# A decoder layer on one core: weights handed over tile by tile, and TensorE's order taken from the scheduler

## The chip, the core and the metric

The kernel runs on one core of a Trainium2 chip. A core has a matrix engine (TensorE, PE in the profile; its weight loads are listed as PEld), three engines for elementwise work (VectorE or DVE, ScalarE or ACT, GpSimd or POOL) and SyncE (SP), which issues all the DMAs of this kernel. Each engine takes its instructions in its own fixed order and waits on semaphores for the others. Matrix products land in PSUM, 8 banks of 128 x 512 float32; everything else works in SBUF. The metric is the device time of one execution in microseconds (us).

## The reference, cut to what matters

```python
def reference(x, c, w_ada, b_ada, g_attn, w_in, b_f, sinks, w_out,
              g_mlp, w_up, conv_w, conv_b, w_down, g_final):
    mod = jax.nn.silu(c) @ w_ada + b_ada
    sh1, sc1, ga1, sh2, sc2, ga2 = jnp.split(mod, 6, axis=-1)
    h = modulate(rms_norm(x, g_attn), sh1, sc1)
    x = x + ga1[:, None, :] * hybrid_mixer(h, w_in, b_f, sinks, w_out)
    h2 = modulate(rms_norm(x, g_mlp), sh2, sc2)
    x = x + ga2[:, None, :] * conv_glu_mlp(h2, w_up, conv_w, conv_b, w_down)
    return rms_norm(x, g_final)
```

x is 2048 rows of 1024 float32. The mixer projects h with w_in (1024 x 2312) into queries, keys and values of 8 heads with a sliding window of 128 and of 8 heads of forgetting attention over all earlier rows, and multiplies the heads by w_out (1024 x 1024). The MLP is h2 @ w_up (1024 x 5632), a causal convolution of width 3, silu(g) * a, and a product with w_down (2816 x 1024). w_ada is 1024 x 6144.

## The kernel before

**Tiles and stages.** The 2048 rows are cut into four blocks n = 0..3 of 512. For each, s1(n) makes the projections (L276 for the first groups of block 0, L623 for the columns q and k, L651 for the values), s2(n) the attention, and s3(n) the rest: the product with w_out (L1183), the normalised rows h2 turned by transposes (L525), the product with w_up (L1301) and the one with w_down (L1183 again). Each dense product is made of three, of a high and a low part of either side: in a row of the profile, `hh,wh`, `hl,wh`, `hh,wl`.

**Attention.** A unit of forgetting attention (fox_unit) makes scores s (L968), the maximum of each column by a transpose mt (L993), spreads it over rows by mb (L1000), takes exponentials on ACT and differences on DVE (L1018, L1019), sums by a transpose lt (L1039), and multiplies the probabilities, split into ph and pl (L728, L729), with the values into o (L1063, L1066); yo (L1072 to L1074) is its output. There are 8 such units for block 0 and 1, one a head, and 16 for block 2 and 3. The sliding window has its scores at L798, its transposes at L840 and its products at L851 and L852, with yo at L867 and L868.

**Weights.** `want` lists all weight tiles in the order of use, `feed` (L409) loads them some tiles ahead of use from the ten buffers of the tag w, and `split_w` makes wh on ACT (L378) and wl on DVE (L379). Some tiles, once split, are stored to DRAM (L406) and loaded as wkh and wkl for later blocks (L399). A tile of w_up or of w_in's columns is 128 columns of all 1024 rows: SBUF [128, 8, 128]. A tile of w_out, w_down and of w_in's first groups is 256 rows of up to 512 columns: [128, 2, 512]. The values' tiles are two or three blocks of rows of 320 or 328 columns. w_ada comes in 96 tiles of 128 x 512: 32 by `ada_pair` (L191), each of two pieces of 256 columns, at the start, and 64 by `ada_chunk` (L181) while the first attention runs; DVE adds them up (L199, L201), and PE sums them over the partitions (L256, and L209 in `mod_cols`). h2 needs what L209 gives.

**What sets the order.** The last lines of the kernel body `merge` a dense generator (s1, s3) with an attention generator (s2): for each step of dense products that is written out, attention steps are written out as a ratio and a table of gaps allow. So s2(1) is written between the steps of s3(0), s2(2) between those of s1(3) and s3(1), and s2(3) between those of s3(2). The framework's scheduler then plans the whole program with a model of each instruction's duration, and decides the order on each engine; an instruction that is written earlier goes first if both are ready in the plan. For PE this is switched off, for the whole kernel, by

```python
    ctx.enter_context(tc.manual_schedule(engines={mybir.EngineType.PE}))
```

(L117): PE executes its instructions as they were written. Within s1(0)'s first groups DVE and SP are held to the written order too (L608), and DVE at the very end (L1432).

Of the kernel before, what the change touches and what calls it, by code (L numbers as in the profile page):

```python
# [15 lines left out]
P = 128  # L16
D = 1024
# [3 lines left out]
KT = D // P  # L21
# [9 lines left out]
FG = 3  # L31
NW = 1 + (FG > 0)
# [38 lines left out]
def tile_decoder_layer(  # L71
# [4 lines left out]
    w_ada: bass.AP,  # L76
    b_ada: bass.AP,
    g_attn: bass.AP,
    w_in: bass.AP,
    b_f: bass.AP,  # L80
    sinks: bass.AP,
    w_out: bass.AP,
# [8 lines left out]
    nc = tc.nc  # L91
# [22 lines left out]
        return t[:, :w]  # L114

    nc.scalar.preload_act_table_set("exp_and_others")
    ctx.enter_context(tc.manual_schedule(engines={mybir.EngineType.PE}))  # L117

    def side_ps(w=512):
        t = pa.tile([P, 512], F32, tag="s", name="sd", bufs=3)  # L120
# [10 lines left out]
        out=tri, in_=tri, pattern=[[1, P]], compare_op=ALU.is_ge, fill=0.0,  # L131
# [5 lines left out]
        out=cmask, in_=cmask, pattern=[[1, P]], compare_op=ALU.is_ge, fill=-BIG,  # L137
# [8 lines left out]
        out=dist, in_=dist, pattern=[[-1, 256]], compare_op=ALU.is_ge, fill=1e35,  # L146
# [3 lines left out]
        out=dist, in_=dist, pattern=[[1, 256]], compare_op=ALU.is_gt, fill=1e35,  # L150
# [30 lines left out]
    def ada_chunk(i, accs):  # L181
        acc = ap.tile([P, 512], F32, tag="act", name="acc")
        for k in range(KT):
            w = ap.tile([P, 512], F32, tag="act", name="wada")
            with behind():
                nc.sync.dma_start(w, w_ada[k * P : (k + 1) * P, i * 512 : (i + 1) * 512])
            ada_step(acc, w, k)
            yield
        accs.append(acc)

    def ada_pair(i, k, acc):  # L191
        w = at.tile([P, 2, 256], F32, tag="t", name="wada2", bufs=NT)
        src = w_ada[k * P : (k + 1) * P, 0 : 2 * D].rearrange("p (s n) -> p s n", s=2)
        nc.sync.dma_start(w, src[:, :, i * 256 : (i + 1) * 256])
        ada_step(acc, w.rearrange("p s n -> p (s n)"), k)

    def ada_step(acc, w, k):
        if k == 0:
            nc.vector.tensor_scalar(acc, w, cc[:, 0:1], 1.0, ALU.mult, ALU.mult)  # L199
        else:  # L200
            nc.vector.scalar_tensor_tensor(  # L201
                acc, w, cc[:, k : k + 1], acc, ALU.mult, ALU.add
            )
# [32 lines left out]
    def first_groups():  # L236
# [48 lines left out]
        for i in range(5):  # L285
            sums = None
            if i < 4:
                sums = ap.tile([P, 512], F32, tag="act", name="acc")
            for k in range(KT):
                if i < 4:  # L290
                    ada_pair(i, k, sums)
                if i > 0 and k == 1:
                    shape(i - 1, prev)
                    if i > 1:
                        for m in range(1, NW):
                            products(2 * i - 4, [m])
                            products(2 * i - 3, [m])
                if i > 0 and k in (3, 5):
                    kk = 2 * (i - 1) + (k - 3) // 2
                    modulate_one(*h_pair(hh, hl, kk), xts[kk], kk, 0, 0)  # L300
                    if k == 5:
                        products(kk - 1, [0])
                        products(kk, [0])
            prev = sums
            if i == 0:
                feed(3, 2)
# [23 lines left out]
    def prologue_later():  # L330
        for chunks in ((4, 5), range(6, 10), (10, 11)):
            accs = []
            for i in chunks:
                yield from ada_chunk(i, accs)
            for _ in range(MY):
                yield
            if chunks == (4, 5):
                mod_rows(accs, 16, 0)
                late["gate"] = True
            elif chunks == (10, 11):  # L340
                mod_rows(accs, 40, 1)
            else:
                mod_cols(accs, 24)
                nc.vector.scalar_tensor_tensor(
                    scl[:, 8:16], mod[:, 32:40], 1.0, late["gml"], ALU.add, ALU.mult
                )
                late["mod"] = True
# [34 lines left out]
    def behind():  # L382
        return tc.issue_after(flow["last"]) if "last" in flow else nullcontext()
# [6 lines left out]
    def want(shape, srcs, key=None, use=None):  # L390
        if use is not None:
            mode[len(reqs)] = (key, use)
        reqs.append((shape, srcs))
# [42 lines left out]
    def want_s1(n):  # L436
        if n == 0:
            for k2 in range(KT // 2):
                for c0, c1 in ((768, 1280), (1280, 1280 + FG * P))[:NW]:
                    want([P, 2, c1 - c0], [((slice(None),), w_in[  # L440
                        k2 * 256 : (k2 + 1) * 256, c0:c1
                    ].rearrange("(a p) n -> p a n", p=P))])
        cols = []
        for i in range(4):
            if n > 0:
                cols += [768 + i * P, 1280 + i * P]
            elif i >= FG:
                cols += [1280 + i * P]
        def want_cols(cols):
            for col in cols:  # L450
                want([P, KT, P], [((slice(None),), w_in[:, col : col + P].rearrange(
                    "(k p) n -> p k n", p=P))])

        want_cols(cols)
        for ch in range(2):
            wd = 320 + 8 * ch
            for k0, nk in ((0, 3), (3, 3), (6, 2)):
                src = w_in[k0 * P : (k0 + nk) * P, :].rearrange("(k p) n -> p k n", p=P)
                a = slice(None)
                if ch == 0:  # L460
                    srcs = [
                        ((a, a, slice(0, 128)), src[:, :, 640:768]),
                        ((a, a, slice(128, 320)), src[:, :, 1792:1984]),
                    ]
                else:
                    srcs = [((a, a, a), src[:, :, 1984:2312])]
                want([P, nk, wd], srcs)
        want_cols([i * P for i in range(5)])

    def use_of(n, key):  # L470
        if key not in first_use:
            first_use[key] = KEEP[len(first_use) % len(KEEP)]
        at0 = first_use[key]
        return "load" if n > at0 else "store" if n == at0 else "raw"
# [3 lines left out]
    def want_rows(src, order, n, name):  # L478
        for half in range(2):
            for k2 in [k // 2 for k in order if k % 2 == 0]:  # L480
                key = f"{name}{half}_{k2}"
                want([P, 2, 512], [((slice(None),), src[
                    k2 * 256 : (k2 + 1) * 256, half * 512 : (half + 1) * 512
                ].rearrange("(a p) n -> p a n", p=P))], key, use_of(n, key))

    def want_s3(n):
        want_rows(w_out, OUT_ORDER, n, "o")
        calm.update(range(len(reqs) - CB, len(reqs) + CN))
        for f in range(NF):
            for ci in (f, NF + f):  # L490
                key = f"u{ci}"
                want([P, KT, P], [((slice(None),), w_up[:, ci * P : (ci + 1) * P].rearrange(
                    "(k p) n -> p k n", p=P))], key, use_of(n, key))
        want_rows(w_down, range(NF), n, "d")

    def sumsq(row, out, junk=None):
# [1002 lines left out]
    for (kind, n), alt in zip(order, (0, 1, 1, 2, 3, 3, 4, 5)):  # L1499
        if kind == "s1":  # L1500
            want_s1(n)
        else:
            want_s3(n)
        alts.extend([alt] * (len(reqs) - len(alts)))
# [21 lines left out]
_INS = [  # L1526
    "x", "c", "w_ada", "b_ada", "g_attn", "w_in", "b_f", "sinks", "w_out",
    "g_mlp", "w_up", "conv_w", "conv_b", "w_down", "g_final",
]
_OUTS = [((1, S, D), "float32")]  # L1530


# [27 lines left out]
```

## Time and profile before

| | |
|---|---|
| median of 3 runs | 2754.8 us (2751.72 to 2756.76) |
| the profiled execution | 2755.67 us, span 2754.0 us |
| DMA queue of SP | 424316 packets, 585.79 MB, busy 65.8% of 16 engines' span |
| packets under 2 KB | 272756 |

The span is the time from the first to the last instruction. A row of the waits reads: who waited, for whom, then the sum in us, the number of waits and the longest. In a timeline row the time of the start and the duration come first, and in brackets stands how long the engine had been idle and what ended that.

### The profile page before, as it was taken

The numbers are of one execution on the slowest core, as the hardware profiler recorded it, in microseconds if no ns is written. First come the engines' busy times: TensorE is split into PE (matmuls) and PEld (weight loads), VectorE is DVE, ScalarE is ACT, GpSimd is POOL, SyncE is SP. The second block draws the span as 40 slices with busy tenths as digits, with TensorE's granted clock in tenths as the row PEclk, the third lists the DMA queues.
The fourth block names the chain that finished last, engine by engine and source line by source line (L and its number), as shares of the span: only waits on it lengthen the run. The fifth ranks groups of instructions, "written<-read, shape, count | busy, mean of one in ns | idle before, by whom it ended". The sixth has DMA issues, their size and how long they took to land.

```text
span 2754.0 us, 38503 instructions
## 1 busy us (share of the span) xinstructions
PE 2566.3 (93%) x12852; PEld 2168.5 (79%) x12852; DVE 1930.8 (70%) x3813; ACT 1491.7 (54%) x3085; POOL 93.1 (3%) x171
## 2 busy tenths in 40 slices
PE   7999888799989999988999999989999999999998
PEld 5878786677877877877788887878888887788887
DVE  6467656789878657776888865879989876344433
ACT  5456564565556666556555665576666666422222
POOL 0001000100000000000000000100000000000000
PEclk9999999899999999999999999999999999999999
DMA  7967579756646786675667779735555576655564
GB/s 234 296 181 234 153 216 306 237 178 200 198 150 201 218 263 204 210 245 166 211 225 228 236 255 300 274 119 179 182 186 180 180 243 218 249 196 196 188 228 183
DMA packets 424515, 588.26 MB, mean 214 GB/s; under 512 B 32380, under 2 KB 272756, under 8 KB 424316
## 3 DMA queue, kind: packets, MB, share of 16 engines
q1 hardware_dynamic: 424316, 585.79, 65.8%
q8 instruction: 102, 1.67, 0.3%
q14 instruction: 97, 0.79, 0.1%
HBM read 440.95 MB, written 144.71 MB: 213 GB/s over the span
## 4 chain that ended last, share of the span: by engine, by line
PE 75%; DVE 8%; DMA 7%; ACT 5%; issue 2%; SPq 1%; POOL 1%; DVEq 0%; POOLq 0%; ACTq 0%
PE d L1301 33%; PE d L1183 19%; PE d L623 6%; PE s L968 4%; DMA wada<-in_w_ada_dram 2%; PE o L1063 2%; PE o L1066 2%; PE d L651 2%; DVE wl L379 1%; DMA q<-qd 1%; DMA wr<-in_w_in_dram 1%; PE mb L1000 1%; PE d L276 1%; PE s L798 1%; DVE pl L729 1%
## 5 line engine op out<-in xcount | busy, mean ns | idle before, releaser
L1301 PE MATMUL d<-hh,wkh 128*128 128x512 f32 (+1 forms) x920 | 355.4, 386 | 6.3 <-ACT hh L110 6.3
L1301 PE MATMUL d<-hl,wkh 128*128 128x512 f32 (+1 forms) x920 | 354.7, 386 | 3.7 <-DVE hl L538 2.7
L1301 PE MATMUL d<-hh,wkl 128*128 128x512 f32 (+1 forms) x920 | 352.1, 383 | 0.0
L379 DVE TENSOR_TENSOR wl<-wr,wh 128x1024 fp32r<-128x1024 f32 (+5 forms) x184 | 219.2, 1192 | 113.9 <-ACT wh L378 99.4
L728 ACT CAST ph<-t 128x512 fp32r<-128x512 f32 (+2 forms) x304 | 178.2, 587 | 188.8 <-PE o L1063 185.9
L378 ACT CAST wh<-wr 128x1024 fp32r<-128x1024 f32 (+5 forms) x184 | 188.5, 1025 | 169.0 <-PE d L1301 78.6
L985 ACT ACTIVATE t<-s,bc 128x256 f32<-128x256 f32 (+3 forms) x464 | 204.5, 480 | 103.3 <-DVE t L979 49.7
L1331 ACT ACTIVATE u<-d,cb,cw 128x512 f32<-128x512 f32 x176 | 136.7, 777 | 223.2 <-PE d L1301 217.7
L1334 DVE SCALAR_TENSOR_TENSOR u<-d,cw,u 128x511 f32<-128x511 f32 x176 | 130.8, 743 | 158.9 <-ACT u L1331 158.2
L729 DVE TENSOR_TENSOR pl<-t,ph 128x512 fp32r<-128x512 f32 (+2 forms) x304 | 195.8, 646 | 37.7 <-ACT ph L728 36.5
L1301 PE MATMUL d<-hh,wh 128*128 128x512 f32 (+1 forms) x552 | 215.7, 391 | 2.2 <-ACT hh L110 2.2
L1301 PE MATMUL d<-hl,wh 128*128 128x512 f32 (+1 forms) x552 | 214.2, 388 | 0.4
L968 PE MATMUL s<-q,kkb 128*128 128x256 f32 (+2 forms) x1024 | 198.6, 309 | 16.8 <-DMA q<-qd 16.8
L1301 PE MATMUL d<-hh,wl 128*128 128x512 f32 (+1 forms) x552 | 213.1, 386 | 0.0
L1301 PEld LDWEIGHTS d<-hh,wkh 128*128 128x128 f32 x920 | 174.4, 190 | 39.3 <-ACT hh L110 8.8
L1301 PEld LDWEIGHTS d<-hl,wkh 128*128 128x128 f32 x920 | 174.1, 189 | 38.1 <-DVE hl L538 7.5
L1301 PEld LDWEIGHTS d<-hh,wkl 128*128 128x128 f32 x920 | 174.2, 189 | 33.5
L1063 PE MATMUL o<-ph,vvb 128*128 128x256 f32 (+2 forms) x512 | 153.9, 318 | 27.7 <-DVE yo L1073 27.7
L1019 ACT ACTIVATE t<-t 128x512 f32<-128x512 f32 (+2 forms) x304 | 168.5, 598 | 13.4 <-DVE t L1018 7.2
L968 PEld LDWEIGHTS s<-q,kkb 128*128 128x128 f32 x1024 | 153.7, 197 | 24.5 <-DMA q<-qd 16.4
L623 PE MATMUL d<-hh,wh 128*128 128x512 f32 x360 | 146.2, 406 | 2.6 <-DVE lf L666 2.2
L623 PE MATMUL d<-hl,wh 128*128 128x512 f32 x360 | 143.9, 400 | 2.9 <-DVE hl L538 2.9
(232 smaller groups left out, 6128.5 us busy)
## 6 DMA issues: line engine op xcount, KB each, us to landing
wkh<-wsu SPq DMA_DIRECT2D x110, 512.0 KB
wkl<-wsu SPq DMA_DIRECT2D x110, 512.0 KB
wr<-in_w_up_dram SPq DMA_DIRECT2D x66, 512.0 KB
wkh<-wsd SPq DMA_DIRECT2D x55, 512.0 KB
wkl<-wsd SPq DMA_DIRECT2D x55, 512.0 KB
wr<-in_w_in_dram SPq DMA_DIRECT2D x49, 512.0 KB
wada<-in_w_ada_dram SPq DMA_DIRECT2D x96, 256.0 KB
wsu<-wh SPq DMA_DIRECT2D x44, 512.0 KB
```

The costliest lines, as they stand in the source:

```text
L378: nc.scalar.copy(wh, raw)
L379: nc.vector.tensor_sub(wl, raw, r32(wh))
L623: nc.tensor.matmul(ps, a[:, k, :], b[k], start=(k == 0 and i == 0), stop=(k == KT - 1 and i == 2),)
L728: nc.scalar.copy(ph[:, e0:], src[:, e0:])
L729: nc.vector.tensor_sub(pl[:, e0:], src[:, e0:], r32(ph[:, e0:]))
L968: nc.tensor.matmul(ps[:, o + low(c0) : o + w], st["kks"][kb // 4][:, (kb % 4) * P : (kb % 4 + 1) * P], qs[a][:, low(c0) : w], start=(a == ...
L985: nc.scalar.activation(tt[:, plain : o + w], ps[:, plain : o + w], AF.Identity, bias=bias(kb))
L1019: nc.scalar.activation(t1, t1, AF.Exp)
L1063: nc.tensor.matmul(po[:, c:], v, ph[:, o + c : o + w], start=(kb == 0), stop=False)
L1183: nc.tensor.matmul(acc[t], l[:, ts], r[:, k % 2, :], start=(i == 0 and l is ah and r is wh), stop=(i == n_k - 1 and l is al),)
L1301: nc.tensor.matmul(ps[:, c], w[a][:, k, :], b[k][:, c], start=(k == 0 and i == 0), stop=(k == KT - 1 and i == 2),)
L1331: nc.scalar.activation(u, ps, AF.Identity, bias=cb[:, ci : ci + 1], scale=c2)
```

## The change

The weights are laid out anew before they are handed to the kernel: each tile lies in one piece in DRAM, in the order in which its partitions hold it. w_in is handed over as five arrays, so that the two pieces of a values' tile, which came from two places, come as one. No value changes and no load is dropped but for the second DMA of these twelve tiles. And the line that held PE to the written order is gone.

```diff
     nc.scalar.preload_act_table_set("exp_and_others")
-    ctx.enter_context(tc.manual_schedule(engines={mybir.EngineType.PE}))
...
-                nc.sync.dma_start(w, w_ada[k * P : (k + 1) * P, i * 512 : (i + 1) * 512])
+                nc.sync.dma_start(w, w_ada[i, k])
...
-                for c0, c1 in ((768, 1280), (1280, 1280 + FG * P))[:NW]:
-                    want([P, 2, c1 - c0], [((slice(None),), w_in[
-                        k2 * 256 : (k2 + 1) * 256, c0:c1
-                    ].rearrange("(a p) n -> p a n", p=P))])
+                for w in (w_in_h0, w_in_h1)[:NW]:
+                    want([P, 2, w.shape[3]], [((slice(None),), w[k2])])
...
-                want([P, KT, P], [((slice(None),), w_in[:, col : col + P].rearrange(
-                    "(k p) n -> p k n", p=P))])
+                want([P, KT, P], [((slice(None),), w_in_c[col // P - (col > 640)])])
...
-                if ch == 0:
-                    srcs = [
-                        ((a, a, slice(0, 128)), src[:, :, 640:768]),
-                        ((a, a, slice(128, 320)), src[:, :, 1792:1984]),
-                    ]
-                else:
-                    srcs = [((a, a, a), src[:, :, 1984:2312])]
+                srcs = [((slice(None),), (w_in_v0, w_in_v1)[ch][:, k0 : k0 + nk, :])]
...
-                want([P, 2, 512], [((slice(None),), src[
-                    k2 * 256 : (k2 + 1) * 256, half * 512 : (half + 1) * 512
-                ].rearrange("(a p) n -> p a n", p=P))], key, use_of(n, key))
+                want([P, 2, 512], [((slice(None),), src[half, k2])], key, use_of(n, key))
...
-                want([P, KT, P], [((slice(None),), w_up[:, ci * P : (ci + 1) * P].rearrange(
-                    "(k p) n -> p k n", p=P))], key, use_of(n, key))
+                want([P, KT, P], [((slice(None),), w_up[ci])], key, use_of(n, key))
...
+    def columns(w):
+        return w.reshape(KT, P, -1, P).transpose(2, 1, 0, 3)
+    def rows(w):
+        return w.reshape(-1, 2, P, 2, 512).transpose(3, 0, 2, 1, 4)
+    def head(w):
+        return w.reshape(KT // 2, 2, P, -1).transpose(0, 2, 1, 3)
+    def by_partition(w):
+        return w.reshape(KT, P, -1).transpose(1, 0, 2)
```

`columns` serves w_up and w_in_c, `rows` w_out and w_down, `head` w_in_h0 and w_in_h1, and `by_partition` w_in_v0 and w_in_v1; the array for w_ada is put together in the same manner, a tile after the other.

What the change moves stands in no table: it is what the scheduler decides now. In both kernels PE has the same instructions; before, each follows the one that was written before it, and now 2,230 of some 12,800 do not. Two places on PE follow. In the changed kernel these lines stand 12 lower: 1289 is L1301, 1051 and 1054 are L1063 and L1066, 988 is L1000, 956 is L968, 1027 is L1039, 981 is L993, 513 is L525; 211 is L209.

The first place is s3(0), where s2(1) is woven into the products with w_up. On PE before, an attention product o stands between two dense products:

```order
L1301 MATMUL d<-hh,wh 128x512
L1301 MATMUL d<-hl,wh 128x512
L1301 MATMUL d<-hh,wl 128x512
L1063 MATMUL o<-ph,vvb 128x512
L1066 MATMUL o<-pl,vvb 128x512
L968 MATMUL s<-q,kkb 128x512 x2
```

And PE now, at the same o (the last row):

```order
L988 MATMUL mb<-ident,rl 128x128 x4
L956 MATMUL s<-q,kkb 128x512 x2
L1289 MATMUL d<-hh,wl 128x512
L1289 MATMUL d<-hh,wh 128x512
L1289 MATMUL d<-hl,wh 128x512
L1289 MATMUL d<-hh,wl 128x512
L1289 MATMUL d<-hh,wh 128x512
L1289 MATMUL d<-hl,wh 128x512
L1289 MATMUL d<-hh,wl 128x512
L1289 MATMUL d<-hh,wh 128x512
L1289 MATMUL d<-hl,wh 128x512
L1051 MATMUL o<-ph,vvb 128x512
```

23 matrix instructions that were written behind this o stand ahead of it now, dense ones nearly all; the rows mb and s above are of earlier attention steps and have moved back.

The second place is the end of the product with w_out in s3(0), where PE sums w_ada's accumulators (L209, 16 columns) and turns the rows (L525) for h2. On PE before:

```order
L209 MATMUL sd<-ones,acc 128x1 x16
L1063 MATMUL o<-ph,vvb 128x512
L1066 MATMUL o<-pl,vvb 128x512
L968 MATMUL s<-q,kkb 128x512 x2
L1039 MATMUL lt<-ident,acc 128x128 x4
L1063 MATMUL o<-ph,vvb 128x384
L1066 MATMUL o<-pl,vvb 128x384
L993 MATMUL mt<-ident,mx 128x128 x4
L968 MATMUL s<-q,kkb 128x512 x2
L1063 MATMUL o<-ph,vvb 128x256
L1066 MATMUL o<-pl,vvb 128x256
L525 MATMUL d<-ident,x1row 128x128 x6
```

And PE now:

```order
L211 MATMUL sd<-ones,acc 128x1 x8
L956 MATMUL s<-q,kkb 128x512 x2
L1027 MATMUL lt<-ident,acc 128x128 x2
L981 MATMUL mt<-ident,mx 128x128 x2
L1027 MATMUL lt<-ident,acc 128x128 x2
L981 MATMUL mt<-ident,mx 128x128 x2
L956 MATMUL s<-q,kkb 128x512 x2
L211 MATMUL sd<-ones,acc 128x1 x4
L988 MATMUL mb<-ident,rl 128x128 x4
L988 MATMUL mb<-ident,m 128x128 x4
L211 MATMUL sd<-ones,acc 128x1 x4
L956 MATMUL s<-q,kkb 128x512 x6
```

The 16 sums of L209 come in three pieces, with scores and transposes of attention between them; the products o and the six transposes x1row, which stood behind, stand ahead of the first piece.

More of the change, by code (lines that the diff above doesn't have):

```diff
@@ L78, in tile_decoder_layer @@
     g_attn: bass.AP,
-    w_in: bass.AP,
+    w_in_c: bass.AP,
+    w_in_v0: bass.AP,
+    w_in_v1: bass.AP,
+    w_in_h0: bass.AP,
+    w_in_h1: bass.AP,
     b_f: bass.AP,
@@ L192, in ada_pair @@
         w = at.tile([P, 2, 256], F32, tag="t", name="wada2", bufs=NT)
-        src = w_ada[k * P : (k + 1) * P, 0 : 2 * D].rearrange("p (s n) -> p s n", s=2)
-        nc.sync.dma_start(w, src[:, :, i * 256 : (i + 1) * 256])
+        nc.sync.dma_start(w, w_ada[i, k].rearrange("p (s n) -> p s n", s=2))
         ada_step(acc, w.rearrange("p s n -> p (s n)"), k)
@@ L457, in want_s1 @@
             for k0, nk in ((0, 3), (3, 3), (6, 2)):
-                src = w_in[k0 * P : (k0 + nk) * P, :].rearrange("(k p) n -> p k n", p=P)
-                a = slice(None)
-                if ch == 0:
-                    srcs = [
-                        ((a, a, slice(0, 128)), src[:, :, 640:768]),
-                        ((a, a, slice(128, 320)), src[:, :, 1792:1984]),
-                    ]
-                else:
-                    srcs = [((a, a, a), src[:, :, 1984:2312])]
+                srcs = [((slice(None),), (w_in_v0, w_in_v1)[ch][:, k0 : k0 + nk, :])]
                 want([P, nk, wd], srcs)
@@ L1529, with _laid_out @@
 ]
+def _laid_out(inputs, np):
+    def columns(w):
[6 more added lines that the diff above has]
+        return w.reshape(KT, P, -1).transpose(1, 0, 2)
+    out = {}
+    for name in _INS:
+        a = np.asarray(inputs[name])
+        if name == "w_ada":
+            first = a[:, : 2 * D].reshape(KT, P, 2, 4, 256).transpose(3, 0, 1, 2, 4)
+            rest = a[:, 2 * D :].reshape(KT, P, 8, 512).transpose(2, 0, 1, 3)
+            out[name] = np.concatenate([first.reshape(4, KT, P, 512), rest])
+        elif name == "w_in":
+            out["w_in_c"] = columns(np.concatenate([a[:, :640], a[:, 768:1792]], axis=1))
+            out["w_in_v0"] = by_partition(np.concatenate([a[:, 640:768], a[:, 1792:1984]], axis=1))
+            out["w_in_v1"] = by_partition(a[:, 1984:2312])
+            out["w_in_h0"] = head(a[:, 768:1280])
+            out["w_in_h1"] = head(a[:, 1280 : 1280 + FG * P])
+        elif name in ("w_out", "w_down"):
+            out[name] = rows(a)
+        elif name == "w_up":
+            out[name] = columns(a)
+        else:
+            out[name] = a
+    return {name: np.ascontiguousarray(a) for name, a in out.items()}
 _OUTS = [((1, S, D), "float32")]
@@ L1542 @@
     )
-    arrays, args = {}, []
-    for name in _INS:
-        a = _np.ascontiguousarray(inputs[name])
+    arrays, args = {}, {}
+    for name, a in _laid_out(inputs, _np).items():
         arrays[f"in_{name}_dram"] = a
-        args.append(
-            nc.dram_tensor(
-                f"in_{name}_dram", a.shape, _mybir.dt.from_np(a.dtype), kind="ExternalInput"
-            ).ap()
-        )
+        args[name] = nc.dram_tensor(
+            f"in_{name}_dram", a.shape, _mybir.dt.from_np(a.dtype), kind="ExternalInput"
+        ).ap()
     for i, (shape, dtype) in enumerate(_OUTS):
         dt = _mybir.dt.from_np(_np.dtype(dtype))
-        args.append(nc.dram_tensor(f"out_{i}_dram", shape, dt, kind="ExternalOutput").ap())
+        args["out"] = nc.dram_tensor(f"out_{i}_dram", shape, dt, kind="ExternalOutput").ap()
     with _tile.TileContext(nc, schedule_with_timeline_sim=True) as tc:
-        tile_decoder_layer(tc, *args)
+        tile_decoder_layer(tc, **args)
     r = _run(nc, [arrays], core_ids=[0])
```

## The prediction

> **What bounds the kernel now.** I read the cores view and the page first, then the busy time by stage, then who made TensorE (PE) wait, and last the timeline at the longest of those waits.
>
> ```profile
> core 0: 2754.0 us, clock 0.967
> ```
>
> ```profile
> span 2754.0 us, 38503 instructions
> PE 2566.3 (93%) x12852; PEld 2168.5 (79%) x12852; DVE 1930.8 (70%) x3813; ACT 1491.7 (54%) x3085; POOL 93.1 (3%) x171
> ```
>
> PE is the bound: it is busy 2566.3 of 2754.0 us, so 187.7 us are left in which it does nothing, and its granted clock is 0.967 and not 1. Nothing else is near a full span. The stages say where the 187.7 us lie (the columns after the stage: its length, busy time of each engine with its instructions, granted clock, DMA share, GB/s):
>
> ```profile
> 0.00:550.00 550.00, 473.09 (x2404) 403.06 (x2405) 351.24 (x765) 297.05 (x613) 39.23 (x69) 0.93 0.76 233
> 550.00:1101.00 551.00, 513.50 (x2410) 424.08 (x2409) 428.25 (x777) 334.22 (x656) 10.86 (x25) 0.96 0.65 201
> 1101.00:1377.00 276.00, 252.13 (x1372) 219.64 (x1371) 202.64 (x406) 152.19 (x314) 10.09 (x15) 0.96 0.64 208
> 1377.00:1790.00 413.00, 402.55 (x2048) 340.55 (x2047) 324.17 (x643) 248.65 (x534) 11.55 (x17) 0.99 0.78 253
> 1790.00:2409.00 619.00, 588.68 (x3144) 503.03 (x3143) 486.01 (x993) 382.03 (x848) 16.40 (x38) 0.98 0.58 193
> 2409.00:2754.00 345.00, 336.32 (x1484) 278.15 (x1482) 138.52 (x233) 77.59 (x122) 4.98 (x8) 0.99 0.55 198
> ```
>
> Length minus PE's busy time gives 76.9, 37.5, 23.9, 10.5, 30.3 and 8.7 us of idle. Three fifths of it is in the first 1101 us, where the clock is lowest too; the last 345 us are dense products alone and have next to none. Who ends the waits:
>
> ```profile
> PE o L1063 <- DVE yo L1073: 27.7, 9, 7.5
> PE mt L993 <- DVE mx L959: 20.9, 12, 4.5
> PE s L968 <- DMA q<-qd: 16.8, 4, 10.1
> PE sd L209 <- DVE acc L201: 14.3, 2, 8.7
> PE o L851 <- DVE yo L868: 11.6, 7, 4.0
> PE sd L525 <- ACT xrow L110: 11.5, 4, 6.3
> PE d L651 <- DVE vst L663: 9.4, 8, 2.4
> PE d L1301 <- ACT hh L110: 8.5, 13, 3.5
> PE mt L993 <- DVE mx L951: 5.8, 2, 5.0
> PE mt L993 <- ACT hraw L533: 3.7, 1, 3.7
> ```
>
> Most rows are attention (o, mt, s) that stands at a fixed place in PE's queue while the dense products behind it could run. That is a wait of order, not of work.
>
> **PE's order, wait by wait.** The change leaves PE's instructions and their sizes alone and moves them. For each wait of over 1 us I took the waiting instruction from the timeline and counted in the new order what now stands ahead of it that stood behind it. A dense 128x512 product takes 0.227 us in a row of its kind (5.44 / 24):
>
> ```profile
> 609.94 5.44 PE d L1301 x24
> ```
>
> The longest ones:
>
> ```profile
> 481.04 0.77 PE L968 MATMUL s<-q,kkb 128*128 128x512 f32 x1 [10.14 <-DMA q<-qd]
> 678.21 0.77 PE L1063 MATMUL o<-ph,vvb 128*128 128x512 f32 x1 [5.99 <-DVE yo L1073]
> 1247.69 0.58 PE L1063 MATMUL o<-ph,vvb 128*128 128x256 f32 x1 [7.47 <-DVE yo L1073]
> 521.82 1.86 PE L209 MATMUL sd<-ones,acc 128*128 128x1 f32 x8 [5.57 <-DVE acc L201]
> 532.40 1.86 PE L209 MATMUL sd<-ones,acc 128*128 128x1 f32 x8 [8.71 <-DVE acc L201]
> ```
>
> At 481.04, 52 instructions have come ahead, some 11.3 us of PE: the 10.14 us are covered. At 678.21 it is 23, 5.2 us with the narrow ones at their width: 5.2 of 5.99 covered. At 1247.69 it is ten, 1.1 us: 6.4 us stay. Of the two waits at L209, about 3.3 us are covered by the attention rows between its pieces; the dense products there need its result. In the same way, as the smaller of the wait and of what came ahead: o behind yo (L1063) 15.5 of 27.7; mt behind L959 13.8 of 20.9; s behind q 14.0 of 16.8; o behind L868 5.7 of 11.6; the row transposes 2.0 of 11.5; L651 3.9 of 9.4; L1301 1.6 of 8.5; mt behind L951 5.0 of 5.8; mt behind hraw all 3.7. With L209's 3.3 that is 68.5 us; I take **68**. The other rows (each under 7 us) I leave out. Below, this term is bounded by 0 (the plan's work is not ready on the chip when it is called), above by all 187.7 less the start's waits, some 170.
>
> **The clock behind these waits.** Right after the covered waits the clock stands at half. The stretches behind thirteen of them, the first and the last, and the sum row of all:
>
> ```profile
> 246.00:249.00 3.00, 3.00 (x10) 2.91 (x11) 1.05 (x5) 0.57 (x2) 0.29 (x1) 0.50 0.96 277
> 2157.00:2160.00 3.00, 3.00 (x10) 2.32 (x9) 2.74 (x6) 3.00 (x7) 0.00 (x0) 0.51 0.91 279
> sum 65.00, PE 49.83 PEld 40.94 DVE 40.85 ACT 20.24 POOL 0.58; mean PE 3.83 PEld 3.15 DVE 3.14 ACT 1.56 POOL 0.04
> ```
>
> PE is busy for 49.83 us there at half speed; at full speed the same work takes half: **25 us** go with the waits. Bounds: 0, if other waits as long appear, and 0.033 x 2754 = 91 us, the whole loss of the clock.
>
> **New waits.** In the new order attention comes as soon as the plan has its inputs ready, with no cushion. The trace has a price for one such wait, the recurring 1.52 us ahead of a column maximum:
>
> ```profile
> 1937.99 0.44 PE L993 MATMUL mt<-ident,mx 128*128 128x128 f32 x2 [1.52 <-DVE mx L959]
> ```
>
> I take one for each of the eight forgetting-attention heads that run between 550 and 1101 us, where most of the covered waits behind the start lie: +12 us. Bounds: 0, and the slower rival below.
>
> **The layout.** A w_up tile and a w_in column tile came as 1024 pieces of 512 B and now come as 128 pieces of 4 KB; w_ada's pairs, the row tiles of w_in, w_out and w_down double their piece; twelve tiles that took two DMAs take one. Bytes stay.
>
> ```profile
> wr<-in_w_up_dram SPq DMA_DIRECT2D x66, 512.0 KB
> wr<-in_w_in_dram SPq DMA_DIRECT2D x49, 512.0 KB
> ```
>
> The DMA view from 550 to 900 us, where w_up is loaded in small pieces, against 2409 to 2616, where nearly all pieces are 4 KB (packets, MB, share of 16 engines):
>
> ```profile
> q1 hardware_dynamic: 66021, 64.30, 59.8%
> ```
>
> ```profile
> q1 hardware_dynamic: 10947, 39.86, 53.3%
> ```
>
> 64.30 MB in 0.598 x 350 us is 307 GB/s while busy, 39.86 MB in 0.533 x 207 us is 361. A 512-KB tile falls from 1.71 to 1.45 us, and the 111 tiles that came in 512-B pieces give back 29 us of the 16 engines' time. It lies beside other work: the DMA share is 0.55 to 0.78 in all stages, and in the rows above PE waits for a DMA itself only for q. What could come to the path is the wait for w_ada, which L209 inherits:
>
> ```profile
> DVE acc L201 <- DMA wada<-in_w_ada_dram: 55.0, 23, 6.3
> ```
>
> Only the first 32 of its 96 loads change their pieces; the start's chain of eight saves at most 8 x (0.85 - 0.73) = 1 us. I take **-1 us**, between 0 and -29. The Trainium skill speaks against even that: DMA: Bandwidth & Descriptors, section Specifications, gives 512 B as the least transfer for line-rate, so that 512-B pieces would lose nothing. By that the layout gives 0, and the sum is 1 us more. The trace doubts the rule (307 against 361 GB/s), though the two stretches differ in more than their pieces.
>
> **The sum.** The profiled execution took 2755.67 us, 1.67 more than its span, and lies 0.9 us above the median 2754.8 of three. 2755.7 - 68 - 25 + 12 - 1 = **2674 us**, 2.9% less. DVE's share in 550 to 1101 goes from 428 of 551 to 428 of about 520 us, 82%; in 1858 to 2134 it is at 253 of 276 already and the kernel lives with that:
>
> ```profile
> 1858.00:2134.00 276.00, 268.41 (x1462) 230.70 (x1462) 253.08 (x508) 171.27 (x365) 1.85 (x9) 1.00 0.54 181
> 2134.00:2340.00 206.00, 200.24 (x1043) 169.55 (x1043) 158.88 (x341) 131.84 (x313) 6.37 (x11) 0.99 0.66 214
> ```
>
> There up to 167 instructions come ahead of a waiting mt, and attention falls behind the dense products before it catches up; that costs nothing as long as DVE's 47 free us in 2134 to 2340 take what was put off.
>
> **Rivals.**
> 1. *More is filled than I count.* The rows left out, half of the start and all of the clock behind them go too. For it: the plan has moved work at nearly every wait. Against it: the 6.29 us before the first transposes and the dense chain at the start have nothing to fill them. 2674 - 45 = about 2630 us.
> 2. *Half comes back.* DVE, ACT and the single SP queue follow the same plan; where PE stops waiting for yo, it waits for the splits of the weights or of the probabilities (L379, L729), which sit in DVE's queue. The gain halves: about 2715 us.
> 3. *Slower: no cushion.* PE runs strictly in its order, so a hand-off (mt, mb, o) that the chip has ready later than planned stops all dense products behind it. There are 48 forgetting-attention units with three such hand-offs, 144. At 1 us each beyond plan that is +144 in place of my +12: 2806 us. It is slower than before from 0.65 us each (94 / 144). For it: the 1.52 us above recur though a cushion was written in. Against it: lateness of one hand-off makes the next less late, and the plan found the same waits that the trace shows.
> 4. *It does nothing.* The waits return at other places one for one and the layout is hidden: 2752 us.
>
> **How the numbers follow.** Forecast as summed 0.62 (its own range 2640 to 2710), rival 1 0.13, rival 2 0.11, rival 3 0.09, rival 4 0.05. Faster is the first three, 0.86; within 0.2%, about what a measurement of this kernel can tell from no change, 0.05; slower 0.09. The range takes in rivals 1 and 2 and the most of 4: 2605 to 2750 us; it leaves out the full clock term together with all waits below, and rival 3 above.
>
> **What will show it.** PE's idle time falls from 187.7 to about 120 us; the waits of s for q, and of mt for L951, are gone, and o behind yo is near 12 us; the granted clock rises to about 0.976; the first 1101 us of work shrink by some 60 us, and the last 345 us stay. Pieces under 2 KB fall by over 100,000 while PE's sum of busy time moves by the clock alone. I am wrong if PE shows many new waits of 1 to 3 us on mt, mb or o in the middle stages, if DVE's share passes 95% there, or if dense products wait for wh or wl.

## The result, and the profile after

The changed kernel takes 2665.0 us (median of 4 runs, 2660.1 to 2668.8), the kernel before in the same session 2755.8 (2751.7 to 2761.7): a ratio of 0.9674, 95% interval 0.9653 to 0.9695. That is 90 us, 3.3%, and 9 us less than the forecast 2674. The profiled execution took 2663.1 us.

The cores view of the changed kernel, and four lines of its page (span, busy time of each engine, DMA packets by size, SP's queue):

```profile
core 0: 2661.4 us, clock 0.976
```

```profile
span 2661.4 us, 38402 instructions
PE 2544.1 (96%) x12852; PEld 2155.2 (81%) x12852; DVE 1918.8 (72%) x3813; ACT 1472.0 (55%) x3085; POOL 91.7 (3%) x171
...
DMA packets 304769, 588.24 MB, mean 221 GB/s; under 512 B 32188, under 2 KB 137396, under 8 KB 304572
q1 hardware_dynamic: 304572, 585.79, 65.8%
```

PE's idle time is 2661.4 - 2544.1 = 117.3 us, where it was 187.7: 70.4 us less. Its busy time fell by 22.2 us with the same 12852 instructions, and the granted clock rose from 0.967 to 0.976: that part goes with the clock. The two make the 92.6 us by which the span is shorter. They are read from one execution of each kernel; over all those on record the clock of the kernel before lay between 0.967 and 0.973, that of the changed one between 0.973 and 0.977, so another pair would split the gain somewhat differently. SP's queue moved the same 585.79 MB in 0.658 x 2661.4 = 1751 us of its engines' time, before in 0.658 x 2754.0 = 1812.

The windows view of the changed kernel, cut at the same places of the work as the stages of before (length, busy time of each engine with its instructions, granted clock, DMA share, GB/s):

```profile
0.00:527.00 527.00, 478.13 (x2492) 410.81 (x2493) 362.00 (x794) 306.56 (x643) 35.36 (x69) 0.95 0.75 244
527.00:1028.00 501.00, 496.47 (x2388) 413.15 (x2387) 416.50 (x757) 320.27 (x632) 11.17 (x25) 0.99 0.68 223
1028.00:1303.00 275.00, 266.51 (x1454) 231.78 (x1453) 221.56 (x446) 163.80 (x342) 12.56 (x16) 0.98 0.67 225
1303.00:1677.00 374.00, 367.57 (x1873) 310.06 (x1871) 286.64 (x576) 222.84 (x487) 7.76 (x15) 0.99 0.78 260
1677.00:2318.00 641.00, 600.68 (x3176) 512.51 (x3176) 495.04 (x1013) 380.96 (x862) 19.90 (x38) 0.96 0.56 188
2318.00:2661.00 343.00, 334.76 (x1477) 276.85 (x1476) 137.03 (x230) 77.59 (x122) 4.97 (x8) 0.99 0.55 198
```

The second row is the gain at its clearest: 37.5 us of idle have become 4.5, at a clock of 0.99 instead of 0.96. The fifth is the other side: 641 us where there were 619, with 40 us of idle instead of 30, at 0.96 instead of 0.98. A finer cut, at the first dense product of each stage in the timeline, says where (us):

| stage | before | after | gain |
|---|---|---|---|
| s1(0), s1(1), s1(2) | 421.1 | 391.7 | 29.4 |
| w_out(0) | 92.7 | 93.3 | -0.6 |
| up(0), the products with w_up | 329.2 | 294.3 | 34.9 |
| down(0) | 169.2 | 158.0 | 11.2 |
| s1(3) | 134.3 | 123.7 | 10.6 |
| w_out(1) | 80.5 | 65.0 | 15.5 |
| up(1), down(1), w_out(2) | 549.8 | 542.7 | 7.1 |
| up(2) | 352.3 | 352.6 | -0.3 |
| down(2), w_out(3) | 220.0 | 238.2 | -18.2 |
| up(3), down(3) | 377.0 | 374.1 | 2.9 |

So some 109 us are gained in six places, and one stage gives 18 back. Who ends PE's waits now, the first rows of that view and two further down:

```profile
PE d L513 <- ACT x1row L114: 14.5, 4, 7.6
PE sd L513 <- ACT xrow L114: 10.0, 4, 6.3
PE o L1054 <- DVE pl L717: 8.7, 12, 1.4
PE d L1289 <- DVE halo L1333: 8.7, 3, 3.3
...
PE mt L981 <- DVE mx L939: 1.6, 2, 0.9
...
PE o L1051 <- DVE yo L1061: 0.9, 2, 0.8
```

Of o behind yo, the longest row of before with 27.7 us, 0.9 are left. What stands first now are the transposes of normalised rows (L513). New among them is the halo row: dense products of w_up that wait for DVE's convolution.

### The profile page after: what moved, and what is told of

Its sections match the earlier page's. It is cut to its first block, busy times and chain, and to the rows that moved or that the text cites. A ratio compares the mean times of both kernels' runs of the same rounds, so it can differ in the third digit from the quotient of the medians.

```text
span 2661.4 us, 38402 instructions
## 1 busy us (share of the span) xinstructions
PE 2544.1 (96%) x12852; PEld 2155.2 (81%) x12852; DVE 1918.8 (72%) x3813; ACT 1472.0 (55%) x3085; POOL 91.7 (3%) x171
## 2 busy tenths in 40 slices
DMA packets 304769, 588.24 MB, mean 221 GB/s; under 512 B 32188, under 2 KB 137396, under 8 KB 304572
## 3 DMA queue, kind: packets, MB, share of 16 engines
q1 hardware_dynamic: 304572, 585.79, 65.8%
## 4 chain that ended last, share of the span: by engine, by line
PE 83%; DVE 5%; DMA 5%; ACT 4%; issue 2%; POOL 1%; SPq 1%; POOLq 0%; DVEq 0%; ACTq 0%
PE d L1289 36%; PE d L1171 21%; PE d L611 8%; PE s L956 4%; PE d L639 3%; PE o L1054 2%; PE o L1051 2%; PE d L278 1%; PE mb L988 1%; DVE t L1002 1%; PE s L786 1%; DMA yraw<-yd 1%; DMA q<-qd 1%; DMA wada<-in_w_ada_dram 1%; PE pt L828 1%
## 5 line engine op out<-in xcount | busy, mean ns | idle before, releaser
L1054 PE MATMUL o<-pl,vvb 128*128 128x256 f32 (+2 forms) x512 | 146.7, 306 | 8.7 <-DVE pl L717 8.7
```

Source lines behind the costliest of these rows:

```text
L1054: nc.tensor.matmul(po[:, c:], v, pl[:, o + c : o + w], start=False, stop=(kb == nkb - 1))
```

## The experiments

All ten ran in five rounds beside the kernel before, so the ratios compare, not the raw times: that kernel's median was 2748.9 us beside the first four, 2746.2 beside the next four and 2750.0 beside the last two. The times that the expectations name count from the session of the result, where that kernel took 2755.8 us. Line numbers in rows of an experiment are its own, a few off from the changed kernel's.

**1. The layout alone, the order alone.** The first keeps the new layout and holds PE to the written order; the second is the kernel before without its line.

```diff
  layout alone: the changed kernel
+    ctx.enter_context(tc.manual_schedule(engines={mybir.EngineType.PE}))
  order alone: the kernel before
-    ctx.enter_context(tc.manual_schedule(engines={mybir.EngineType.PE}))
```

> The weights are handed over as tiles, and PE keeps the written order. Theory 'order': the layout lies beside other work, so the time is that of the kernel before less 1 to 5 us, about 2752 us; PE's idle time stays near 187 us while the DMA queue's busy time falls by about 60 us (65.8% of 2754 to 65.8% of 2661 us). Rival 'layout': the loads that land earlier are what shortens the start and the w_ada sums; then 2735 us or less, and DVE's 55 us of waits for w_ada at least halve.

> The weights stay as before (512-B pieces), and PE's order is left to the scheduler. Theory 'order': nearly all of the gain, about 2668 us, PE idle near 118 us, clock 0.975. Rival 'layout': 2685 us or more.

Measured: layout alone 2744.9 us, ratio 0.9989 (0.9976 to 1.0002); order alone 2673.1, ratio 0.9719 (0.9703 to 0.9736). The order carries 2.81%, 77 us of 2754.8, which is less than expected: by its ratio order alone is at 2678 us of 2755.8, between the 2668 of the theory and the 2685 of its rival, with 124.5 us of idle and a clock of 0.972. "Order" means the whole plan here: without the line, some 2,100 of VectorE's 3813 instructions and 1,400 of ScalarE's 3085 follow another one than before (by the order of start in the traces), and no run frees PE while it holds the others. With the order held, the layout is worth 3 us, which is not told apart from nothing; with the order free, the difference from order alone to both (0.9719 to 0.9674) is 12 us, with intervals that just miss each other (the two were measured in different sessions). By these numbers the two parts don't add up; they work on each other. The page of the layout alone shows that its DMA time went all the same:

```profile
q1 hardware_dynamic: 304572, 585.79, 64.0%
```

0.640 x 2750.0 is 1760 us of queue time, 52 less than before, and next to none of it reached the end while PE stood in its written order. The 52 is rough: the eight kernels with all tiles laid out anew and every load in place took 1732 to 1760 us of queue time, the two in the old layout 1805 (order alone) and 1812.

**2. Block 2 held, block 2 free.** The loss lies where s2(3) is merged into s3(2). One kernel holds PE's order there alone, the other everywhere ahead of it.

```diff
  block 2 held: the changed kernel
-    merge(s3(2, [lambda: yprep(3, 1)]), s2(3), RM[3] * att_cost(3) / 383.0)
+    with tc.manual_schedule(engines={mybir.EngineType.PE}):
+        merge(s3(2, [lambda: yprep(3, 1)]), s2(3), RM[3] * att_cost(3) / 383.0)
  block 2 free: the changed kernel
+    with tc.manual_schedule(engines={mybir.EngineType.PE}):
         (the four merges ahead of that one)
```

> The changed kernel, but PE keeps the written order where s3(2) and s2(3) are merged. Theory 'lead': there the scheduler lets the dense products run ahead, attention is put off, and in the products with w_down(2) and w_out(3) DVE and ACT must make it up: this stage took 238.3 us after and 220.0 before. Held to the written order it is back to 220, and the kernel takes 2665 - 18 = 2647 us. Rival 'join': the loss comes from the row work at the start of s3(3) (loads of y, rows of x) now that all before it is shorter; then it stays, 2665 us.

> The changed kernel with PE held to the written order everywhere up to the merge of s3(2) and s2(3), and free from there. Theory 'lead': the free order only harms here, 2752 + 18 = 2770 us. Rival 'join': no loss, 2752 us or less, since its 30 us of idle time are filled.

Measured: held 2644.4 us, ratio 0.9622 (0.9608 to 0.9637); free 2766.4, ratio 1.0065 (1.005 to 1.0079). In the first, down(2) with w_out(3) is back at 219.5 us and all else keeps its gain to within 4 us. Its windows row for the stage:

```profile
2049.00:2268.00 219.00, 211.73 (x1072) 178.09 (x1070) 148.20 (x311) 129.70 (x310) 8.80 (x16) 0.99 0.72 240
```

The second has the loss without the gains, and is slower than the kernel before by 18 us (14 to 22 by the interval). So the same freedom that wins in the early stages loses in this one, and either comes without the other.

**3. Up(2) held, down(2) held.** The stage that is longer need not be the one in which the harm is done. The windows view of before and then of the changed kernel, up(2) first and down(2) with w_out(3) second:

```profile
1805.00:2157.00 352.00, 338.60 (x1864) 291.20 (x1864) 316.48 (x636) 221.61 (x474) 2.26 (x11) 0.99 0.52 175
2157.00:2377.00 220.00, 211.95 (x1075) 178.21 (x1073) 148.56 (x313) 129.98 (x312) 9.48 (x18) 0.99 0.72 240
```

```profile
1696.00:2049.00 353.00, 336.36 (x1814) 288.50 (x1814) 299.61 (x606) 206.23 (x452) 2.05 (x10) 0.97 0.51 172
2049.00:2287.00 238.00, 224.59 (x1134) 188.19 (x1134) 168.22 (x354) 143.07 (x343) 9.06 (x18) 0.97 0.68 226
```

In up(2) the free order does 50 PE instructions and 16.9 us of DVE's work less than the held one, in the same time; in the next stage it does 59 and 19.7 us more. Attention has slid behind. Two kernels ask in which of the two stages the freedom costs:

```diff
+    def hold(stage, n):
+        while holding:
+            holding.pop().__exit__(None, None, None)
+        if (stage, n) in HELD:
+            h = tc.manual_schedule(engines={mybir.EngineType.PE})
+            h.__enter__()
+            holding.append(h)
...
+        hold("up", n)
         for f in range(NF):
...
  up(2) held:    HELD = {("up", 2)}
  down(2) held:  HELD = {("down", 2), ("out", 3)}
```

> The changed kernel with TensorE's order held to the program's in up(2) alone (the loop over the 22 column pairs of block 2 and the attention of block 3 merged into it); down(2) and w_out(3) stay free. Theory 'lead': the free order lets attention fall behind in up(2) (DVE 299.6 us busy there against 317.2 with the order held), and the 18.3 us lost in down(2)+w_out(3) are the price, paid later. Then holding up(2) alone brings them back: 2665 - 18 + 1 = 2648 us (2641 to 2654), down(2)+w_out(3) 219 to 223 us. Rival 'place': the loss is made by the free order inside down(2)+w_out(3) itself; then it stays, 238 us there and 2663 to 2669 us in all.

> The changed kernel with TensorE's order held in down(2) and w_out(3) alone; up(2) stays free. Theory 'lead': what up(2) put off is still to be done, and a held order puts it all where it stood, ahead of the products that could run: 235 to 245 us in down(2)+w_out(3), 2660 to 2672 us in all. Rival 'place': 219 to 223 us there, 2645 to 2650 us in all.

Measured: up(2) held 2639.0 us, ratio 0.9611 (0.9598 to 0.9624), by which it is 2649 of 2755.8, as theory 'lead' had it; down(2) held 2664.5, ratio 0.9704 (0.9688 to 0.972), 2674 of 2755.8 and near the upper end of what 'lead' gave. The windows view of the two, the same two stages:

```profile
1694.00:2046.00 352.00, 340.78 (x1871) 294.05 (x1872) 318.86 (x642) 223.70 (x481) 2.25 (x11) 0.98 0.51 173
2046.00:2263.00 217.00, 212.05 (x1078) 177.82 (x1076) 148.81 (x317) 128.57 (x313) 8.89 (x17) 1.00 0.73 247
```

```profile
1698.00:2050.00 352.00, 335.81 (x1814) 288.90 (x1813) 298.96 (x605) 205.84 (x449) 2.05 (x10) 0.97 0.50 172
2050.00:2294.00 244.00, 225.08 (x1135) 190.46 (x1135) 170.81 (x355) 145.25 (x345) 9.77 (x19) 0.96 0.66 221
```

With up(2) held, the next stage takes 217 us though it is free. With down(2) held and up(2) free, it takes 244 us: the put-off attention is still there (1135 PE instructions against 1078), and the held order is no help with it. The debt is made in up(2) and paid in down(2). What PE waits for in up(2) says how it is made; first the changed kernel, then the one with up(2) held:

```profile
PE d L1289 <- DVE halo L1333: 8.7, 3, 3.3
PE o L1054 <- DVE pl L717: 2.9, 3, 1.2
PE o L1051 <- ACT ph L716: 2.7, 2, 2.2
```

```profile
PE mt L993 <- DVE mx L959: 7.6, 5, 1.5
PE d L1303 <- DVE hl L526: 2.6, 5, 0.8
```

The free order avoids the 1.5-us waits of mt by taking dense products instead, and these then run ahead of DVE's convolution and wait for it, three times for 2.4 to 3.3 us. In all PE is idle for 16.6 us there against 11.2 with the order held, at a clock of 0.97 against 0.98. So up(2) does less work and is no shorter, and attention is late at its end.

**4. w_in alone in the old layout.** Which of the new tiles matter, once PE is free? This kernel hands w_in over as before and the four other weights as tiles; PE's instructions stand in the changed kernel's order, and by the traces VectorE's and ScalarE's too, but for a dozen places. The same holds for order alone.

```diff
-                want([P, KT, P], [((slice(None),), w_in_c[col // P - (col > 640)])])
+                want([P, KT, P], [((slice(None),), w_in[:, col : col + P].rearrange(
+                    "(k p) n -> p k n", p=P))])
...
```

> The changed kernel with w_in alone handed over as before (column tiles in 512-byte pieces, twelve tiles in two DMAs); w_ada, w_out, w_up and w_down as tiles; TensorE's order is the changed kernel's, instruction for instruction. With TensorE free, the layout was worth 8.4 us in s1(0..2) (400.1 us with the old layout, 391.7 with the new). If w_in's pieces are the cause: s1(0..2) 398 to 402 us, 2672 us in all (2669 to 2676), queue time up by 25 to 35 us of its 1760. If w_ada's pairs are (or the other order that the scheduler chose with them): s1(0..2) 390 to 394 us, 2663 to 2668 us in all.

Measured: 2673.9 us, ratio 0.9736 (0.9718 to 0.9754), 17 us above the changed kernel by the ratios and no better than order alone (0.9719). By its ratio that is 2683 of 2755.8, above the expected 2669 to 2676, but s1(0..2) took 401.5 us, as expected if w_in's pieces are the cause. So w_in's pieces carry what the layout gives, and w_ada's pairs, w_out, w_up and w_down give nothing that shows. Only some 10 of the 17 us lie in s1(0..2), where these tiles are loaded (in order alone, with 400.1 us, it is 8); the rest is spread over later stages, and no run says what makes it. The queue's part of the expectation missed: over the whole run its time is 0.656 x 2677.6 = 1756 us, up by 5 and not by 25 to 35, and inside the 1732 to 1760 of the kernels with all tiles new; in s1(0..2) alone it is up by 12 (0.746 x 402 against 0.735 x 391, by the DMA view). How it gets to PE is in the waits of ACT in that stage; the changed kernel first:

```profile
ACT wh L380 <- DMA wr<-in_w_in_c_dram: 20.2, 8, 6.8
...
ACT wh L380 <- DMA wr<-in_w_in_v_dram: 9.7, 4, 4.7
```

```profile
ACT wh L376 <- DMA wr<-in_w_in_dram: 37.7, 16, 7.1
```

The two views list 29.9 us of waits for w_in's loads against 37.7. In the kernel before, with the old pieces and PE held, the same wait was shorter still:

```profile
ACT wh L378 <- DMA wr<-in_w_in_dram: 15.0, 7, 4.4
```

ACT makes wh, DVE makes wl from it, and what stands behind these on the two engines comes later too. PE itself waits for no weight's load; its wait that grew most in the stage is on DVE, again the changed kernel first:

```profile
PE d L639 <- DVE ql L576: 2.9, 1, 2.9
```

```profile
PE d L646 <- DVE ql L583: 5.4, 3, 4.3
```

The stage's windows show the rest, first the changed kernel's, then this one's:

```profile
28.00:419.00 391.00, 377.68 (x2024) 328.34 (x2024) 263.28 (x611) 226.75 (x485) 18.57 (x41) 0.99 0.74 234
```

```profile
28.00:430.00 402.00, 382.80 (x2026) 332.06 (x2026) 264.83 (x612) 227.85 (x487) 18.89 (x41) 0.97 0.75 229
```

Idle 13.3 against 19.2 us, busy 377.7 against 382.8 at the lower clock: 11 us. That these come from ACT's longer waits for the loads is read from the rows; no run tests that path by itself.

**5. Half of a sum left out.** w_out(0) kept its 93 us, though the wait of 10.14 us and the two at L209 were gone from it. This kernel leaves out half of the products behind the MLP's shift and scale (the upper half of w_ada's rows in its chunks 6 to 9).

```diff
         for k in range(KT):
+            if 6 <= i < 10 and k >= KT // 2:
+                yield
+                continue
             w = ap.tile([P, 512], F32, tag="act", name="wada")
```

> The changed kernel without half of the load and sum of w_ada's chunks 6 to 9 (leaves out half of the products that make the shift and scale ahead of the MLP: 16 tiles of 256 KB and 16 DVE steps of 0.75 us). w_out(0) took 93.3 us after and 92.7 before, though waits of 10.1 and 14.3 us were covered in it. Theory 'sum': w_out(0) ends with this sum, which the load of the tiles (4.2 MB at 293 GB/s, 14 us) and DVE's 12 us draw out; then it falls to 79 to 85 us and the whole to 2651 to 2657. Rival 'rows': the stage ends with the row work of x1 (its loads, gate, sum of squares), and stays at 90 to 93 us, 2661 to 2666 in all.

Measured: 2651.2 us, ratio 0.9653 (0.964 to 0.9666); w_out(0) 73.0 us, a larger fall than expected, so this sum is in what ends the stage. The changed kernel's trace agrees: the scale that is made of the sum (scl, on DVE) comes at 510.7 us, and the first product with w_up at 512.7. It need not be alone in it: the chain that ended last in the stage spends 13.8% of its time in w_ada's loads and 8.8% in the steps of the sum on DVE, but also 8.4% in the rows' root mean squares on POOL. Of the 20 us, 8 are PE's busy time (75.65 us in the changed kernel and 67.75 now, with 17 instructions fewer and a clock of 0.90 in place of 0.81). The whole fell by 6 us only by the ratios (0.9674 to 0.9653), to 2660 of 2755.8, which lies between the ranges of theory and rival; the two intervals overlap, so a gain in all is not shown. Up(0) went from 294.3 to 302.7 us. The windows of w_out(0) and up(0), the changed kernel first:

```profile
419.00:513.00 94.00, 75.65 (x318) 59.78 (x317) 78.02 (x136) 47.66 (x92) 9.97 (x9) 0.81 0.87 293
513.00:807.00 294.00, 294.00 (x1418) 245.10 (x1418) 262.15 (x471) 174.19 (x323) 1.39 (x6) 1.00 0.59 199
```

```profile
418.00:491.00 73.00, 67.75 (x301) 55.41 (x299) 58.34 (x102) 38.28 (x75) 7.78 (x9) 0.90 0.90 317
491.00:794.00 303.00, 301.12 (x1434) 250.89 (x1435) 273.44 (x492) 182.37 (x343) 1.23 (x6) 0.98 0.57 194
```

Up(0) of the changed kernel is full: PE busy for 294.00 of 294 us at a clock of 1.00. Attention that no longer fits beside the sum (17 PE instructions fewer in w_out(0), 16 more in up(0)) has to be paid there: 7.1 us more of PE's busy time, of which 16 instructions at the stage's mean of 0.21 us would be 3.3 (an estimate) and the rest goes with a clock of 0.98 in place of 1.00; and 1.9 us of idle.

**6. The sum earlier.** Both hold up(2), and weave a tile of w_ada into s1(1) and s1(2) at every 6th or 4th step in place of every 8th.

```diff
-    merge(woven(chain(s1(1), s1(2)), late["extra"], 8), s2(0), RM[0] * att_cost(0) / 190.0)
+    merge(woven(chain(s1(1), s1(2)), late["extra"], 6), s2(0), RM[0] * att_cost(0) / 190.0)
```

> TensorE's order held in up(2), and a tile of w_ada woven into s1(1) and s1(2) at every 6th event instead of every 8th, so that more of its sum is done before w_out(0). Theory 'sum' (w_out(0) ends with the sum of w_ada, as the run with half of it left out showed: 73.0 us against 93.3): w_out(0) falls by the moved tiles' share, to 80 to 87 us; s1 has DMA to spare (0.74 of it used) and grows by 0 to 4 us; ratio to the kernel before 0.957 to 0.960 where holding up(2) alone gave 0.9611. Rival 'given back': with less time for attention in w_out(0), up(0) grows by what w_out(0) loses (it went from 294.3 to 302.7 us in that run), and the DMA of s1 is met: 0.960 to 0.965.

> The same with every 4th event: nearly all of w_ada's sum that w_out(0) waited for lies in s1 then. Theory 'sum': w_out(0) 70 to 80 us, s1 plus 3 to 10 us, since its own loads and these tiles share the DMA; ratio 0.954 to 0.960. Rival 'given back': s1 over 402 us or up(0) over 303 us, ratio 0.960 to 0.966.

Measured: at every 6th 2643.8 us, ratio 0.9614 (0.96 to 0.9628); at every 4th 2639.3, ratio 0.9596 (0.9581 to 0.9611). The first missed: w_out(0) stayed at 94.2 us, with 30 of the sum's steps on DVE still in it where the changed kernel has 34, and up(0) took 295.0: nothing was won that could be given back. In the second, 22 steps were left and w_out(0) took 67.3 us:

```profile
429.00:496.00 67.00, 61.41 (x293) 50.31 (x291) 57.18 (x99) 34.91 (x67) 2.86 (x5) 0.96 1.03 354
```

The scale was made 17 us before the stage's end there (478.4 us, the first product with w_up at 496.0), so something else ends it by then. s1 took 400.9 us (10 more than with up(2) held alone) and up(0) 305.2 (10 more): of 25 us won, 20 are given back, as the rival had it, though the ratio lies in the range of theory 'sum'. It is the lowest of all, but its interval overlaps that of up(2) held alone (0.9611), so the 4 us between them are not shown. All three kernels with up(2) held beat the kernel before and the changed one: up(2) held alone by 0.6% of the time before against the changed kernel (0.9611 to 0.9674, and the intervals do not touch).

## Why the prediction was right, and where it was not

**The covered waits, -68 us, and the clock behind them, -25 us.** The mechanism held: PE stood in a written order while work behind it was ready, and with the waits went time at a low clock. The sizes held in the sum only. Two lines of the page of order alone, then of up(2) held:

```profile
span 2673.8 us, 38426 instructions
PE 2549.3 (95%) x12852; PEld 2159.5 (81%) x12852; DVE 1919.4 (72%) x3813; ACT 1470.8 (55%) x3085; POOL 92.5 (3%) x171
```

```profile
span 2636.8 us, 38432 instructions
PE 2537.0 (96%) x12852; PEld 2152.4 (82%) x12852; DVE 1919.7 (73%) x3813; ACT 1474.6 (56%) x3085; POOL 91.9 (3%) x171
```

Of the 70.4 us of idle and the 22.2 us that go with the clock, order alone has 63.2 (187.7 - 124.5) and 17.0 (2566.3 - 2549.3). With up(2) held, idle is 99.8 us. The waits and the clock were to give 93 us. Order alone gave 77 by its ratio (73 to 82 by the interval) and had 21 us of loss in it, since down(2) with w_out(3) took 240.8 us there against 220.0: 98 us ahead of the loss.

**Wait by wait** the count of what had come ahead was a weak guide, and that its sum came so near is in part luck. The ten rows of waits that the prediction shows make 130.2 us before; by the same names 17.6 us of them are left, so that 113 us went where I had 68. All other rows of PE's waits grew together from 47.1 to 90.1 us, by 43 where I had +12: o behind pl and w_up's products behind halo are new, with 8.7 us each, and d behind x1row has grown to 14.5 us from this row of the kernel before:

```profile
PE d L525 <- ACT x1row L110: 5.2, 3, 2.6
```

113 less 43 is the 70 us by which PE's idle time fell. A wait can come back under another name, so this is a count by rows and not by cause. Of o behind yo my count left 12 us, and the trace has 0.9; that a wait covered early brings later inputs in time would explain it, but no run tested that. At 481.04 it had the whole 10.14 us covered, and that wait is gone, but the stage did not end sooner: the sum of w_ada is in what ends w_out(0), as the fifth experiment shows. A covered wait was worth nothing in a stage that ends with something else than PE's work.

**The new waits, +12 us, were put in the wrong place and made too small.** I had them between 550 and 1101 us, where the trace now shows 4.5 us of idle in all. The cost came in the merge of s2(3) into s3(2), 18 us. The step that failed is the sentence that what attention puts off in 1858 to 2134 "costs nothing as long as DVE's 47 free us in 2134 to 2340 take what was put off". DVE did take it, 168 of 238 us busy, and the stage was 18 us longer all the same. I had asked for room on DVE alone, but PE had none: in down(2) with w_out(3) it was busy for 211.95 of 220 us before. What was put off brought it 59 more instructions, 12.6 us more of its busy time (224.59 - 211.95, at a clock of 0.97 where it was 0.99), and 5.4 us more of idle; and up(2), which was rid of 50 instructions, was no shorter for it. So the sum of the order, forecast at -81 us and measured at -77, came out close because waits and clock gave 5 us more and the loss took 9 more: two errors of opposite sign, which is luck.

**The layout, -1 us, was mis-sized.** With the order held the layout gave 3 us, not told from nothing, which agrees with the term. With the order free it is 12 us by the difference to order alone and 17 by the kernel with the old w_in (8 and 10 of them in s1(0..2)), all inside my bound of 29. I had looked for a load that PE itself waits for, and found only q. The load comes to PE in two steps, through ACT's wh and DVE's wl. As I read it, the waits of order hid that: ACT waited 15.0 us for these loads in s1(0..2) while PE was held, and 37.7 with PE free and the same pieces. The whole ends 9 us below the forecast because the layout gave some 12 where I had 1; the order alone would have missed by 4 the other way. The queue time that the new pieces give back was some 52 us (layout alone) where I had worked out 29 for the tiles that came in 512-B pieces alone. Of the rule in the Trainium skill, DMA: Bandwidth & Descriptors, section Specifications, that 512 B is enough for line-rate, this trace says that it does not quite hold here, by some 3%: the same bytes took 1812 us of queue time with 272756 packets under 2 KB, and 1760 us with 137396 of them (layout alone, PE held in both), though every piece of a weight had 512 B or more in both.

**The rivals.** That more is filled than I counted is what the rows show, 113 us for 68, and that a part comes back is so too, 43 us in other rows; by stages, one gives back 18 us of the 109 that the others gain, a sixth and not the half. "No cushion" did not come: the largest row of its hand-offs is o behind pl, 8.7 us in 12 waits, 0.7 each. Slower was possible, though: block 2 freed alone makes a kernel that is slower than before, by another mechanism than the one I named, dense products that run ahead and attention that is late.

**The marks.** Idle about 120 us: 117.3, though 120 had left out my own +12. Clock about 0.976: 0.976. The waits of s for q and of mt for its maximum gone: 0.3 and 1.6 us are left. O behind yo near 12 us: 0.9. The first 1101 us shorter by some 60: by 73. The last 345 the same: 343. Packets under 2 KB down by over 100,000: by 135,360. Of the signs of being wrong none came: waits of 1 us or more on mt, mb and o are 9 in the whole trace where they were 22, DVE is busy for 416.5 of 501 us in the second stretch, 83%, and no row of PE's waits names wh or wl.

## What to carry to other kernels

An engine that runs strictly in its order and is idle for 7% of the span beside ready work can gain by a better order, here by about a third more than the idle time, since the clock rose with it; what each stage gains is limited by what else ends it. A free order can be wrong in one stage and right in the others, so compare busy time and instruction counts stage by stage: a stage that does less work in the same time has put off a debt, and it is there, not where the time is lost, that the order has to be held. A load that PE does not seem to wait for is looked for one and two engines further back, and its worth is measured again once the waits in front of it are gone.

## What the runs showed of the hardware that I had not expected

The granted clock rises as PE's idle time falls, for the same 12852 instructions: 187.7 us of idle with a clock of 0.967 and 2566.3 us busy, 117.3 with 0.976 and 2544.1, 99.8 with 0.979 and 2537.0 with up(2) held. The two are not tied one to one: block 2 free had 188.1 us of idle and a clock of 0.962, and block 2 held 109.1 us with 0.983, more idle than up(2) held and a higher clock. In up(0) of the changed kernel PE was busy for 294.00 of 294 us, and the granted clock there was 1.00.
